# Where y waits for its turn: loading four chunks of y into the halves of four kept tiles, and the first attention gates later

## The chip, the cores and the metric

The kernel runs on one core of one Trainium2 chip. The metric is the device time of one execution in microseconds (us), the median of several runs. Beside it there is one profiled execution, whose trace gives the start and length of every instruction and transfer.

## The reference, cut to what matters

One block of a decoder for 1024 tokens of width 1024, in float32. Only the second branch's projection and what runs beside it matter here:

```python
h = rmsnorm(x, norm_g[l]) * (1.0 + scale[:, None, :]) + shift[:, None, :]
proj = h @ w_in[l]
q, k, v, g_attn, xr, g_rnn, m_attn, m_rnn = jnp.split(proj, SPLIT_POINTS, axis=-1)
...
y_attn = sliding_window_attention_with_sinks(q, k, v, attn_sinks[l]) * jax.nn.silu(g_attn)
y_rnn = rg_lru(xr, ...) * jax.nn.silu(g_rnn)
merged = (jax.nn.sigmoid(m_attn) * (y_attn @ w_attn_proj[l])
          + jax.nn.sigmoid(m_rnn) * (y_rnn @ w_rnn_proj[l]))
x = x + gate[:, None, :] * (merged @ w_out[l])
```

Each float32 operand is written as a high part (rounded to the format that TensorE multiplies) and a low part, the remainder; a product is three: high by high, low by high, high by low.

## The kernel before, in words

The large input projection (`h @ w_in`) is done by pairs of output chunks (`Pair`), each in seven half-size block products (`product`, one per *slot*, 12 matmuls of 128x512), in place of eight. The products' right-hand sides are quarters of h (`hh`, `hl`: high and low parts) and differences of such quarters. The differences' high parts are the eight tiles `nh`, their low parts the four tiles `nl` from the pool `hx` (each 128 partitions x 2 x 1024, 1 MB). A slot uses one half-row of each of the four `nl` tiles: `NT1` (row 0, left half) in slot s+1 of a pair, `T2` (row 1, right) in s+3, `NT3` (row 0, right) in s+6, `NT4` (row 1, left) in s+7 or s+9.

The last slots overlap with the attention. It goes in 32 *units* (u = 0 to 31, one group of four heads by 128 queries each), written by hand in one order for each engine: the unit's scores (`scores`, tiles `s_ps`, from `qs` and `ks`), then one *piece* of other matrix work, then the transposition (`pt`) and the products with v (`pv`) of earlier units. The pieces of units 0 to 5 are the last six slots (s+2 to s+7 of the last pair); from unit 6 on, 32 pieces are the product y @ w_rnn_proj (`rp_steps`, tiles `rp`, matmuls at line 175). Piece i of `rp_steps` runs in unit i+6; pieces 0 and 1 use y's chunks 6 and 7, pieces 2 and 3 chunks 4 and 5, pieces 4 and 5 chunks 0 and 1, pieces 6 and 7 chunks 2 and 3, and from piece 8 on all of them in turn.

What is loaded in that time is asked for on SP's queue, in the order of the code:

- queries and keys: `load_kq(m)` brings `ks` (384 KB) and `qs` (512 KB) for units 2m and 2m+1. There are two places, so the load of m waits for the scores of unit 2m-3; it stands at the end of that unit. kq2 is needed by unit 4, kq3 by unit 6, kq6 by unit 12.
- y: each chunk has a high and a low part (`yh_d`, `yl_d` in HBM, 512 KB each). Chunk 6 and half of 7 stay on the chip, `load_y` brings the rest: 0 and 7 into quarters of h that are used up, 1 to 5 into the pool `ypool`, which is opened in `rp_steps` in the space of h, `nl` and `nh`.
- weights of the projection: `load_r`, two halves `r` of 256 KB. Gates of the attention: `load_gq(m)`, a 256 KB tile `r` of the same ring of six; `a_prep(m)` multiplies it in.

POOL's queue brings the v tiles (`vb`, `vd`) and stores some gates (`smr_d`). SP works in order. Each of its transfers also waits, by a semaphore of eight that go round, for the transfer eight places before it, so at most eight are under way. After the attention, `m_lo`, `mh`, `ml` and later `xo` take `ypool`'s places.

Of the kernel before, what the change touches and what calls it, by code (L numbers as in the profile page):

```python
# [13 lines left out]
F32R = mybir.dt.float32r  # L14
# [4 lines left out]
ALU = mybir.AluOpType  # L19
# [3 lines left out]
P = 128  # L23
S = 1024
D = 1024
KC = 8
HALF = 512
# [18 lines left out]
SL = [slice(0, HALF), slice(HALF, S)]  # L46
# [9 lines left out]
def tile_hybrid_block(ctx, tc, x, pk, rows, posr, posi, c_row, w_ss, w_gate, w_main, w_v,  # L56
                      w_g, w_ap, w_rp, w_out, out):
    nc = tc.nc
    V, A, G, T = nc.vector, nc.scalar, nc.gpsimd, nc.tensor

    def dma(dst, src, eng=nc.sync):
        dst, src = (a.bitcast(F32) if a.dtype == F32R else a for a in (dst, src))
        return eng.dma_start(dst, src)  # L63

    def f32(ap):
        return ap.bitcast(F32)
# [4 lines left out]
    def pool(st, name, bufs=1, **kw):  # L71
        return st.enter_context(tc.tile_pool(name=name, bufs=bufs, reuse_waits="tile", **kw))
# [64 lines left out]
    yh_d = {c: tc.dram_tile([P, S], F32, name=f"yh_d{c}") for c in range(6)}  # L137
# [4 lines left out]


    hba = ctx.enter_context(tc.tile_pool(name="hba", bufs=1))
    h_ctx = ExitStack()
    hb = h_ctx.enter_context(tc.tile_pool(name="hb", bufs=1))
    b12_ctx = ExitStack()
# [10 lines left out]
                lst.append([a[:, SL[0]], a[:, SL[1]]])  # L158
                full.setdefault(kc, []).append(a[:])
    xx = b12_ctx.enter_context(tc.tile_pool(name="xx", bufs=1, side="right"))  # L160
    hx = h_ctx.enter_context(tc.tile_pool(name="hx", bufs=4))
    xall = [hx.tile([P, 2, S], F32, tag="X", name="xT") for i in range(3)]
    xall.append(xx.tile([P, 2, S], F32, name="xT3"))
    xT = [xall[kc % 4][:, kc // 4, :] for kc in range(KC)]
# [390 lines left out]
    B11 = [(hh[i][0], hl[i][0]) for i in range(4)]  # L555
    B21 = [(hh[i + 4][0], hl[i + 4][0]) for i in range(4)]
    B22 = [(hh[i + 4][1], hl[i + 4][1]) for i in range(4)]
    NT1, NT3, NT4, T2 = [], [], [], []

    def differences(i):  # L560
        b11, b12_ = xT[i][:, SL[0]], xT[i][:, SL[1]]
# [5 lines left out]

    def make_operands(i):
        nl = hx.tile([P, 2, S], F32R, tag="X", name="nl")
        for a in range(2):  # L570
            t = i + 4 * a
            A.copy(nh[t][:], xT[t])
            V.tensor_tensor(out=nl[:, a, :], in0=xT[t], in1=f32(nh[t][:]), op=ALU.subtract)
        NT1.append((nh[i][:, SL[0]], nl[:, 0, SL[0]]))
        NT3.append((nh[i][:, SL[1]], nl[:, 0, SL[1]]))
        NT4.append((nh[i + 4][:, SL[0]], nl[:, 1, SL[0]]))
        T2.append((nh[i + 4][:, SL[1]], nl[:, 1, SL[1]]))

    W = {}
# [121 lines left out]
    def at_slot(t, *steps):  # L701

        for i, st_ in enumerate(steps):
            for one in st_ if isinstance(st_, list) else [st_]:
                fixed.setdefault(t + i, []).append(one)
# [744 lines left out]
    def load_r(e):  # L1450
        src = w_rp[e] if e < KC else w_ap[e - KC]
        R[e] = [load_half(src[:, SL[i]]) for i in range(2)]
# [15 lines left out]
                todo.pop(0)()  # L1468

    def load_y(c):  # L1470
        if c == 0:
            yh[c], yl[c] = [[t[i][0] for i in range(2)] for t in (hh, hl)]
            for i in range(2):
                dma(yh[c][i], yh_d[c][:, SL[i]])
                dma(yl[c][i], yl_d[c][:, SL[i]])
            return
        if c >= 6:
            yh[c], yl[c] = [[y_in[c, b][:, t_] for t_ in SL] if (c, b) in y_in else
                            [hh[2 + i][0] for i in range(2)] for b in range(2)]
            if c == 7:  # L1480
                for i in range(2):
                    dma(yl[c][i], yl_d[c][:, SL[i]])
            return
        h_ = W["yp"].tile([P, S], F32R, tag="Y", name="yh")
        l_ = W["yp"].tile([P, S], F32R, tag="Y", name="yl")
        dma(h_[:], yh_d[c])
        dma(l_[:], yl_d[c])
        yh[c] = [h_[:, SL[0]], h_[:, SL[1]]]
        yl[c] = [l_[:, SL[0]], l_[:, SL[1]]]

    def rp_steps():
        h_ctx.close()
        pb_ctx.close()
        psr = pool(ps_ctx, "psr", space=PSUM, side="right")
        rp_acc.extend(psr.tile([P, S], F32, name=f"rp{i}") for i in range(2))
        W["yp"] = pool(ctx, "ypool", bufs=12)
        W["tout"] = pool(ctx, "tout", bufs=1)
        W["hpool"] = pool(ctx, "hpool", bufs=6)

        def part(c, kc2):  # L1500
            for kc in (2 * kc2, 2 * kc2 + 1):
                W["pe"] = mm_k([rp_acc[c % 2][:, t] for t in SL], (O.get((c, 0)), O.get((c, 1))),
                               kc, xh=yh, xl=yl, ends=(6, 3) if c < 2 else (0, KC - 1))

        def finish(c):
            def f():
                flush()
                t = W["tout"].tile([P, S], F32, tag="rp", name="rp32")
                A.copy(t[:], rp_acc[c % 2][:])
                store(tr_d[c], t[:])  # L1510
            later_a.append(f)
            if "att" not in W:
                do_later()

        seq = [(c, k) for k in (3, 2, 0, 1) for c in range(2)]
        seq += [(c, k) for c in range(2, KC) for k in range(4)]
        load_y(4)
        load_y(5)
        for i, (c, k) in enumerate(seq):
            part(c, k)  # L1520
            if i in (1, 2, 3):
                load_y(i)
            if i in (1, 2):
                prep_r(i - 1, 0)
            if i in (6, 10):
                finish(0 if i == 6 else 1)
            if i >= 8 and k == 1 and c > 2:
                finish(c - 1)
            if i % 4 == 2:
                load_r((i + 2) // 4 + 1)  # L1530
            if i >= 4 and i % 4 < 2:
                prep_r((i + 4) // 4, i % 4)
            yield
        finish(7)
# [151 lines left out]
    while W["slot"] < 7 * (len(pairs) - N_ATT) + 1:  # L1686
# [2 lines left out]

    s_last = 7 * len(pairs) - 7  # L1690
    load_y(6)
    at_slot(s_last + 2, ("N", 0, 0, lambda: load_r(0)), ("N", 0, 0, lambda: load_y(7)),
            ("N", 0, 0, lambda: load_r(1)), ("N", 0, 0, lambda: load_y(0)),
            ("N", 0, 0, lambda: prep_r(0, 1)), ("N", 0, 0, lambda: prep_r(1, 1)))

    def fill():
# [23 lines left out]
    for u in range(32 + 3):  # L1720
        todo = (left - KEEP + (35 - u) // 2) // (35 - u)
        if u < 32:
            scores(u)
            maxima_a(u)
            maxima_d(u)
        if 1 <= u < 33:
            weights_a(u - 1)
        low = [steps_[2] for steps_ in high]
        while high:
            high.pop(0)[1]()  # L1730
        for _ in range(todo):
            piece()
        flush()
        if u % 2 and u // 2 + 2 < 16:
            load_kq(u // 2 + 2)
        if 1 <= u < 33:
            weights_d(u - 1)
        if 2 <= u < 34:
            transposed(u - 2)
        if u >= 3:  # L1740
            values(u - 3)
        if 2 <= u < 34:
            split_a(u - 2)
            split_d(u - 2)
        if u >= 3:
            join_a(u - 3)
            join_d(u - 3)
        if u + 1 < 32:
            sink(u + 1)
        while own_stores:  # L1750
            own_stores.pop(0)()
        if 2 <= u < 34:
            masks(u - 2)
        if 3 <= u < 31:
            load_d(u + 1)
            load_v(u + 1)
        if "hpool" in W:
            for f in low:
                f()
            if late and ("gq", late[0]) in U and u >= loaded[late[0]] + 2:  # L1760
                high.append(a_prep(late.pop(0)))
                high[0][0]()
        do_later()
        if u >= 3 and u % 2 == 0:
            late.append((u - 3) // 2)
        if u >= 2 and len(loaded) < 16 and len(loaded) <= (u - 2) // 2 and (
                len(loaded) - (late[0] if late else (u - 2) // 2) < 2):
            m = len(loaded)
            load_gq(m)
            loaded[m] = u  # L1770
# [62 lines left out]
    for c in range(KC):  # L1833
# [24 lines left out]
        if c < 4:  # L1858
            h, l = A11[c]
            A.copy(h, t[:, LEFT])  # L1860
            V.tensor_tensor(out=l, in0=t[:, LEFT], in1=f32(h), op=ALU.subtract)
        else:
            mh, ml = [ypool.tile([P, S], F32R, tag="Y", name=n_) for n_ in ("mh", "ml")]
            for i in SL:
                A.copy(mh[:, i], t[:, i])
            V.tensor_tensor(out=ml[:], in0=t[:], in1=f32(mh[:]), op=ALU.subtract)
            A12.append((mh[:, LEFT], ml[:, LEFT]))
            A22.append((mh[:, RIGHT], ml[:, RIGHT]))
            a11, a21 = [raw[c - 4][:, i] for i in SL]
            a12, a22 = [t[:, i] for i in SL]  # L1870
            V.tensor_tensor(out=a22, in0=a22, in1=a21, op=ALU.add)
            V.tensor_tensor(out=a21, in0=a11, in1=a21, op=ALU.subtract)
            V.tensor_tensor(out=a11, in0=a22, in1=a11, op=ALU.subtract)
            V.tensor_tensor(out=a12, in0=a12, in1=a11, op=ALU.subtract)
# [222 lines left out]
```

## Time and profile before

| what | us |
|---|---|
| runs | 909.71, 909.88, 911.13 (median 909.88) |
| the profiled execution, its time | 909.71 |
| its span, first to last instruction | 908.0 |
| TensorE (PE) busy | 892.6 (98%) |
| VectorE (DVE) busy | 718.5 (79%) |
| ScalarE (ACT) busy | 569.8 (63%) |
| GpSimd (POOL) busy | 186.8 (21%) |
| DMA | 179.79 MB, mean 198 GB/s |
| mean granted TensorE clock | 0.994 |

Times in the trace count from the span's first instruction. Unit 0's scores start at 557.75, unit 6's at 583.56, unit 12's at 618.35. In a timeline row the columns are the start, the length, the engine, the line, the operation with its output and inputs, a count, and in brackets the idle time before it with what ended that. In a window's row stand PE, PEld (weight loads), DVE, ACT and POOL busy in us, the granted clock as a share of full speed, the mean busy share of the 16 DMA engines, and the GB/s that they moved.

### The profile page before, as it was taken

The page shows a single profiled execution, that of the slowest core. Times are in us where ns is not written, and L with a number is a line of the kernel's source. Part 1 is how long each engine was busy: PE and PEld are TensorE (multiplying, and loading weights), DVE is VectorE, ACT ScalarE, POOL GpSimd, SP SyncE. Part 2 cuts the span into 40 slices and gives each one's busy share as a digit, 9 for nine tenths or more (in the row PEclk, how much of TensorE's full clock was granted, in tenths as well). Part 3 has the DMA queues.
Part 4 walks back from the last instruction along what each step waited for, and adds up shares of the span by engine and source line. Part 5 has one row for each costly group of instructions (what it writes and reads, how often), then busy time and mean ns, then how long its engine had stood idle before and what let it go on. Part 6 is the DMA issues. An engine that isn't in the chain of part 4 may idle for free.

```text
span 908.0 us, 12850 instructions
## 1 busy us (share of the span) xinstructions
PE 892.6 (98%) x4314; PEld 747.0 (82%) x4315; DVE 718.5 (79%) x1063; ACT 569.8 (63%) x1099; POOL 186.8 (21%) x330
## 2 busy tenths in 40 slices
PE   9999999999999999999999999997999999999997
PEld 6789888888888888888888888886888888888786
DVE  6998697989679877897897696996999836578855
ACT  7965564655566865777686974885888732115535
POOL 6430241200000000000000002695887720000000
PEclk9999999999999999999999999998999999999999
DMA  9829489863542374265534347997887379416604
GB/s 360 332 94 284 146 258 294 273 212 128 196 163 105 128 251 144 101 229 165 202 112 167 124 137 227 298 344 193 245 237 221 114 263 362 139 47 232 209 1 185
DMA packets 93829, 179.79 MB, mean 198 GB/s; under 512 B 15506, under 2 KB 36002, under 8 KB 93764
## 3 DMA queue, kind: packets, MB, share of 16 engines
q1 hardware_dynamic: 82336, 164.44, 53.0%
q0 software_dynamic: 11280, 14.27, 5.7%
q8 instruction: 34, 0.56, 0.3%
q14 instruction: 31, 0.25, 0.1%
q10 hardware_dynamic: 148, 0.27, 0.1%
HBM read 121.60 MB, written 57.64 MB: 197 GB/s over the span
## 4 chain that ended last, share of the span: by engine, by line
PE 89%; DMA 4%; DVE 3%; ACT 2%; issue 1%; SPq 0%; ACTq 0%
PE bk L714 48%; PE rp L175 13%; PE pgate L1031 5%; PE out L1900 4%; PE pmain L175 4%; PE s_ps L1354 3%; PE pmain L487 2%; PE bk L487 2%; PE pv L1424 2%; DMA yh<-yh_d 2%; DMA qs<-q_d 1%; PE pt L1388 1%; DMA wo<-wo_d 1%; PE pmain L1603 1%; PE pmain L1601 1%; PE pmain L1602 1%
## 5 line engine op out<-in xcount | busy, mean ns | idle before, releaser
L714 PE MATMUL bk<-nh,wh 128*128 128x512 f32 x368 | 143.3, 389 | 0.0
L714 PE MATMUL bk<-nl,wh 128*128 128x512 f32 x368 | 143.2, 389 | 0.0
L714 PE MATMUL bk<-nh,wl 128*128 128x512 f32 x368 | 98.4, 389 | 0.0
L106 ACT CAST wh<-r 128x512 fp32r<-128x512 f32 x107 | 65.5, 618 | 34.1 <-PE pmain L175 10.4
L112 DVE TENSOR_TENSOR wl<-r,wh 128x512 fp32r<-128x512 f32 x91 | 62.1, 691 | 26.2 <-ACT wh L106 26.1
L714 PEld LDWEIGHTS bk<-nh,wl 128*128 128x128 f32 x368 | 69.1, 188 | 14.3
L714 PEld LDWEIGHTS bk<-nl,wh 128*128 128x128 f32 x368 | 69.1, 188 | 14.3
L714 PEld LDWEIGHTS bk<-nh,wh 128*128 128x128 f32 x368 | 69.1, 188 | 14.2
L63 POOL DMA_DIRECT2D yl_d<-it x1 | 0.6, 568 | 349.7 <-DVE it L1114 349.7
L714 PE MATMUL bk<-hl,wh 128*128 128x512 f32 x184 | 71.6, 389 | 0.0
L714 PE MATMUL bk<-hh,wh 128*128 128x512 f32 x184 | 71.6, 389 | 0.0
L112 DVE TENSOR_TENSOR wl<-ws,wh 128x512 fp32r<-128x512 f32 x76 | 51.8, 684 | 6.8 <-ACT wh L106 6.8
L106 ACT CAST wh<-ws 128x512 fp32r<-128x512 f32 x76 | 45.9, 615 | 8.4 <-DVE ws L736 4.1
L1374 ACT ACTIVATE p<-p,small 128x129 f32<-128x129 f32 x128 | 50.0, 396 | 0.0
L714 PE MATMUL bk<-hh,wl 128*128 128x512 f32 x184 | 49.2, 389 | 0.0
L1354 PE MATMUL s_ps<-ks,qs 128*128 128x256 f32 (+1 forms) x256 | 36.5, 286 | 5.2 <-DMA qs<-q_d 5.2
L714 PEld LDWEIGHTS bk<-hl,wh 128*128 128x128 f32 x184 | 34.6, 188 | 7.2
L714 PEld LDWEIGHTS bk<-hh,wl 128*128 128x128 f32 x184 | 34.5, 188 | 7.2
L714 PEld LDWEIGHTS bk<-hh,wh 128*128 128x128 f32 x184 | 34.5, 188 | 7.1
L1354 PEld LDWEIGHTS s_ps<-ks,qs 128*128 128x128 f32 x256 | 33.6, 195 | 6.8 <-issue 5.6
L175 PE MATMUL rp<-yh,wh 128*128 128x512 f32 x112 | 35.8, 402 | 0.0
L714 PE MATMUL bk<-hha,wh 128*128 128x512 f32 x92 | 35.8, 389 | 0.0
(379 smaller groups left out, 2385.3 us busy)
## 6 DMA issues: line engine op xcount, KB each, us to landing
r<-w_main SPq DMA_DIRECT2D x100, 256.0 KB, 4.3
wada<-w_ss SPq DMA_DIRECT2D x16, 512.0 KB, 9.0
qs<-q_d SPq DMA_DIRECT2D x16, 512.0 KB, 8.0
wo_d<-wr SPq DMA_DIRECT2D x28, 256.0 KB, 4.3
wo<-wo_d SPq DMA_DIRECT2D x14, 512.0 KB, 6.6
ks<-k_d SPq DMA_DIRECT2D x12, 384.0 KB, 6.2
xt<-x SPq DMA_DIRECT2D x8, 512.0 KB, 6.9
sma_d<-c SPq DMA_DIRECT2D x16, 256.0 KB, 4.2
```

The costliest lines, as they stand in the source:

```text
L106: A.copy(dst[0][:], src)
L112: eng.tensor_tensor(out=dst[1][:], in0=src, in1=f32(dst[0][:]), op=ALU.subtract)
L175: mm = T.matmul(ps[hf], ww, xx[kc][hf], start=(kc == ends[0] and ww is w_h and xx is xh), stop=(kc == ends[1] and xx is xl))
L487: T.matmul(starts[c][hf], ww[:, c0:c0 + P], xh[kc][hf], start=(kc == 0 and t_ == "h"), stop=(kc == KC - 1 and t_ == "l"))
L714: W["pe"] = T.matmul(ps, ww[:, kc * P:(kc + 1) * P], b[kc][i], start=(first and n == 0), stop=(n == 11), skip_group_check=not first)
L1031: W["pe"] = T.matmul(ps[:, SL[hf]], ww[:, c0:c0 + P], xx_[:, SL[hf]], start=(ic == 0 and i == 0), stop=(ic == 1 and i == 2))
L1354: W["pe"] = T.matmul(o, qs[:, j, qc], ks[:, kb:n % 2 + 2, b, :], start=(b == 0), stop=(b == 1))
L1374: A.activation(px[:, j, :], px[:, j, :], AF.Exp, bias=sm[:, 0, j:j + 1], accum_out=sm[:, 1, j:j + 1])
L1388: W["pe"] = T.transpose(pt[:, :, j, :], px[:, j, 0:P], ident[:])
L1424: W["pe"] = T.matmul(pv[:, cols], w, t_[:, cols], start=(i == 0), stop=(i == len(m) - 1))
L1601: T.matmul(o, hh[kc][th][:, ts_], wh[:, cols], start=(kc == 0), stop=False)
L1900: T.matmul(o, a[k][x_][:, p * P:(p + 1) * P], b[k][y_][:, cols], start=(first and k == 0 and i == 0), stop=(k == 3 and i == 2), skip_group ...
```

## The change: what it does

The pool `hx` is no longer closed at the start of `rp_steps`, so the four `nl` tiles (now also listed as `NL`) stay allocated to the end, and `ypool` has 4 places instead of 12. y's chunk 4 goes into the `NT1` halves, chunk 5 into the `T2` halves, each in four transfers of 256 KB, as soon as the last slot that reads them has run: in units 1 and 2 instead of 6. Chunks 2 and 3 go into the contiguous `NT3` and `NT4` halves, chunk 1 alone into `ypool`. Chunk 7's half is asked for a unit earlier. The attention's gates are asked for two units later up to unit 13, after which two are asked for in units 14 and 15 each. After the attention `mh` and `ml` are in `NL`.

```diff
     hba = ctx.enter_context(tc.tile_pool(name="hba", bufs=1))
+    hx = ctx.enter_context(tc.tile_pool(name="hx", bufs=4))
     h_ctx = ExitStack()
...
-    hx = h_ctx.enter_context(tc.tile_pool(name="hx", bufs=4))
...
         nl = hx.tile([P, 2, S], F32R, tag="X", name="nl")
+        NL.append(nl)
...
     def load_y(c):
-        if c == 0:
-            yh[c], yl[c] = [[t[i][0] for i in range(2)] for t in (hh, hl)]
...
+        if c == 1:
+            both = [W["yp"].tile([P, S], F32R, tag="Y", name="y") for _ in range(2)]
...
+        if c in (2, 3):
+            both = [NL[2 * c - 4 + b][:].rearrange("p a s -> p (a s)")[:, HALF:HALF + S]
+                    for b in range(2)]
...
+        elif c >= 4:
+            yh[c], yl[c] = [[NL[2 * b + i][:, c - 4, SL[c - 4]] for i in range(2)]
+                            for b in range(2)]
+        else:
+            yh[c], yl[c] = [[t[i][0] for i in range(2)] for t in (hh, hl)]
+        for b, (t, d) in enumerate(((yh[c], yh_d), (yl[c], yl_d))):
+            if (c, b) not in y_in:
                 for i in range(2):
...
+                    dma(t[i], d[c][:, SL[i]])
...
-        W["yp"] = pool(ctx, "ypool", bufs=12)
+        W["yp"] = pool(ctx, "ypool", bufs=4)
...
-        load_y(4)
-        load_y(5)
+        load_y(1)
         for i, (c, k) in enumerate(seq):
             part(c, k)
-            if i in (1, 2, 3):
+            if i in (2, 3):
                 load_y(i)
...
-    at_slot(s_last + 2, ("N", 0, 0, lambda: load_r(0)), ("N", 0, 0, lambda: load_y(7)),
-            ("N", 0, 0, lambda: load_r(1)), ("N", 0, 0, lambda: load_y(0)),
+    at_slot(s_last + 2, [ask_y(7), ask_r(0)], ask_y(4), [ask_r(1), ask_y(5)], ask_y(0),
...
-        if u >= 2 and len(loaded) < 16 and len(loaded) <= (u - 2) // 2 and (
+        if u >= 2 and len(loaded) < 16 and len(loaded) <= (u - (4 if u < 14 else 2)) // 2 and (
...
-            mh, ml = [ypool.tile([P, S], F32R, tag="Y", name=n_) for n_ in ("mh", "ml")]
+            mh, ml = [NL[c - 4][:, a, :] for a in range(2)]
```

How SP's queue moves, first in units 1 to 4 (`ga_d3`: a gate's store; `ks`, `qs`: kq2, then kq3; `hha`, `hla`: places in h). Before:

```order
L63 DMA ga_d3_100<-c_5362 128x2x256
L63 DMA hha2_170<-yl_d7_129 128x512
...
L63 DMA ks_5449<-k_d_83 128x768
L63 DMA qs_5451<-q_d0_93 128x1024
L63 DMA r_5493<-w_rp 128x512
...
L63 DMA ga_d3_100<-c_5442 128x2x256
L63 DMA r_5511<-ga_d0_97 128x512
L63 DMA hha0_162<-yh_d0_117 128x512
...
L63 DMA ks_5552<-k_d_83 128x768
L63 DMA qs_5554<-q_d0_93 128x1024
```

The same place now:

```order
L63 DMA ga_d3_100<-c_5362 128x2x256
L63 DMA nl_779<-yh_d4_121 128x512
...
L63 DMA ks_5453<-k_d_83 128x768
L63 DMA qs_5455<-q_d0_93 128x1024
L63 DMA r_5497<-w_rp 128x512
...
L63 DMA nl_779<-yh_d5_122 128x512
...
L63 DMA ga_d3_100<-c_5444 128x2x256
L63 DMA hha0_165<-yh_d0_117 128x512
...
L63 DMA ks_5558<-k_d_83 128x768
L63 DMA qs_5560<-q_d0_93 128x1024
L63 DMA r_5664<-ga_d0_97 128x512
```

Chunk 4 (four transfers, the first is shown) now stands ahead of kq2 where chunk 7's two stood, chunk 5 ahead of kq3, and the first gate (`r<-ga_d0`) behind kq3 instead of ahead of it.

Then the queue from kq4 to kq6, units 5 to 9. Before (of a pair of transfers the first is shown):

```order
L63 DMA ks_5695<-k_d_83 128x512
...
L63 DMA yh_5780<-yh_d4_121 128x1024
...
L63 DMA yh_5784<-yh_d5_122 128x1024
...
L63 DMA r_5837<-ga_d0_97 128x512
L63 DMA yh_5880<-yh_d1_118 128x1024
...
L63 DMA ks_5884<-k_d_83 128x768
...
L63 DMA yh_5957<-yh_d2_119 128x1024
...
L63 DMA r_5961<-w_rp 128x512
...
L63 DMA r_6004<-ga_d0_97 128x512
L63 DMA yh_6035<-yh_d3_120 128x1024
...
L63 DMA ks_6039<-k_d_83 128x768
```

The same place now:

```order
L63 DMA ks_5701<-k_d_83 128x512
...
L63 DMA y_5785<-yh_d1_118 128x1024
...
L63 DMA r_5838<-ga_d0_97 128x512
L63 DMA ks_5881<-k_d_83 128x768
...
L63 DMA nl_779<-yh_d2_119 128x1024
...
L63 DMA r_5954<-w_rp 128x512
...
L63 DMA r_5997<-ga_d0_97 128x512
L63 DMA nl_1144<-yh_d3_120 128x1024
...
L63 DMA ks_6031<-k_d_83 128x768
...
L63 DMA r_6134<-ga_d0_97 128x512
```

Chunks 4 and 5 (2 MB) are gone from between kq4 and kq5, and one gate of 256 KB from ahead of kq6. TensorE's own order of matmuls stays as it is.

More of the change, by code (lines that the diff above doesn't have):

```diff
@@ L557, in tile_hybrid_block @@
     B22 = [(hh[i + 4][1], hl[i + 4][1]) for i in range(4)]
-    NT1, NT3, NT4, T2 = [], [], [], []
+    NT1, NT3, NT4, T2, NL = [], [], [], [], []
     def differences(i):
@@ L1470, in load_y @@
     def load_y(c):
-        if c == 0:
-            yh[c], yl[c] = [[t[i][0] for i in range(2)] for t in (hh, hl)]
-            for i in range(2):
-                dma(yh[c][i], yh_d[c][:, SL[i]])
-                dma(yl[c][i], yl_d[c][:, SL[i]])
+        if c == 1:
+            both = [W["yp"].tile([P, S], F32R, tag="Y", name="y") for _ in range(2)]
+            yh[c], yl[c] = [[t[:, t_] for t_ in SL] for t in both]
+            for t, d in zip(both, (yh_d, yl_d)):
+                dma(t[:], d[c])
+            return
+        if c in (2, 3):
+            both = [NL[2 * c - 4 + b][:].rearrange("p a s -> p (a s)")[:, HALF:HALF + S]
+                    for b in range(2)]
+            yh[c], yl[c] = [[t[:, t_] for t_ in SL] for t in both]
+            for t, d in zip(both, (yh_d, yl_d)):
+                dma(t, d[c])
             return
@@ L1479, in load_y @@
                             [hh[2 + i][0] for i in range(2)] for b in range(2)]
-            if c == 7:
-                for i in range(2):
[L1482 to L1489, printed above, removed]
+        elif c >= 4:
[5 more added lines that the diff above has]
+            if (c, b) not in y_in:
+                for i in range(2):
+                    dma(t[i], d[c][:, SL[i]])
     def rp_steps():
@@ L1691, in tile_hybrid_block, with ask_y, ask_r @@
     load_y(6)
-    at_slot(s_last + 2, ("N", 0, 0, lambda: load_r(0)), ("N", 0, 0, lambda: load_y(7)),
-            ("N", 0, 0, lambda: load_r(1)), ("N", 0, 0, lambda: load_y(0)),
+    def ask_y(c):
+        return "N", 0, 0, lambda: load_y(c)
+    def ask_r(c):
+        return "N", 0, 0, lambda: load_r(c)
+    at_slot(s_last + 2, [ask_y(7), ask_r(0)], ask_y(4), [ask_r(1), ask_y(5)], ask_y(0),
             ("N", 0, 0, lambda: prep_r(0, 1)), ("N", 0, 0, lambda: prep_r(1, 1)))
@@ L1862, in tile_hybrid_block @@
         else:
-            mh, ml = [ypool.tile([P, S], F32R, tag="Y", name=n_) for n_ in ("mh", "ml")]
+            mh, ml = [NL[c - 4][:, a, :] for a in range(2)]
             for i in SL:
                 A.copy(mh[:, i], t[:, i])
-            V.tensor_tensor(out=ml[:], in0=t[:], in1=f32(mh[:]), op=ALU.subtract)
+            V.tensor_tensor(out=ml, in0=t[:], in1=f32(mh), op=ALU.subtract)
             A12.append((mh[:, LEFT], ml[:, LEFT]))
```

## The prediction

> **What bounds the kernel now.** I read the page first. TensorE (PE) is busy for nearly the whole span, so a change that moves no matmul can only win back idle or slowed time of PE:
>
> ```profile
> PE 892.6 (98%) x4314; PEld 747.0 (82%) x4315; DVE 718.5 (79%) x1063; ACT 569.8 (63%) x1099; POOL 186.8 (21%) x330
> ```
>
> So I read PE's waits next. One is worth naming, and it has a transfer behind it; the next in size is at the start of the kernel:
>
> ```profile
> PE s_ps L1354 <- DMA qs<-q_d: 5.2, 1, 5.2
> PE bk L258 <- DVE warm L260: 1.4, 1, 1.4
> ```
>
> The chain of work that ended last (start, length) passes there from PE to the transfers and back. What it names is y's chunk 2, then the queries of kq6:
>
> ```profile
> 588.57 0.97 PE s_ps L1354 x8
> 590.42 14.90 DMA yh<-yh_d
> 605.34 12.88 DMA qs<-q_d
> 618.35 2.05 PE s_ps L1354 x8
> ```
>
> PE's timeline gives the price. These are the scores of units 4, 6, 10, 11, the matmul before the wait, and the scores of units 12, 13 and 14:
>
> ```profile
> 573.85 1.12 PE L1354 MATMUL s_ps<-ks,qs 128*128 128x256 f32 x8
> 583.56 1.12 PE L1354 MATMUL s_ps<-ks,qs 128*128 128x256 f32 x8
> 603.54 1.12 PE L1354 MATMUL s_ps<-ks,qs 128*128 128x256 f32 x8
> 608.40 1.12 PE L1354 MATMUL s_ps<-ks,qs 128*128 128x256 f32 x8
> 612.77 0.40 PE L1424 MATMUL pv<-plc,vb 128*128 128x512 f32 x1
> 618.35 2.05 PE L1354 MATMUL s_ps<-ks,qs 128*128 128x256 f32 x8 [5.18 <-DMA qs<-q_d]
> 625.76 1.12 PE L1354 MATMUL s_ps<-ks,qs 128*128 128x256 f32 x8
> 630.62 1.12 PE L1354 MATMUL s_ps<-ks,qs 128*128 128x256 f32 x8
> ```
>
> A unit takes 4.86 us (603.54 to 608.40, and 625.76 to 630.62). Unit 12 stands idle for 5.18 us (613.17 to 618.35) and then takes 625.76 - 618.35 = 7.41 us, 2.55 more than its neighbours. The granted clock says why (columns: PE, PEld, DVE, ACT, POOL busy, clock, DMA share, GB/s):
>
> ```profile
> 560.00:565.00 5.00, 5.00 (x27) 4.25 (x26) 4.42 (x8) 2.81 (x11) 0.00 (x0) 1.00 0.28 92
> 565.00:570.00 5.00, 5.00 (x33) 4.42 (x32) 4.08 (x9) 4.37 (x14) 0.19 (x1) 1.00 0.98 353
> 570.00:575.00 5.00, 5.00 (x31) 4.38 (x30) 4.40 (x8) 4.33 (x15) 1.17 (x3) 1.00 0.77 241
> 575.00:580.00 5.00, 5.00 (x32) 4.41 (x31) 4.74 (x10) 3.57 (x13) 3.55 (x9) 1.00 0.98 313
> 580.00:585.00 5.00, 5.00 (x33) 4.41 (x32) 4.63 (x9) 4.81 (x16) 4.80 (x8) 1.00 0.79 264
> 605.00:610.00 5.00, 5.00 (x32) 4.46 (x31) 4.79 (x10) 4.20 (x14) 4.76 (x10) 1.00 1.07 328
> 615.00:620.00 5.00, 1.65 (x8) 1.68 (x9) 1.81 (x4) 0.00 (x0) 3.45 (x6) 0.70 1.06 271
> 620.00:625.00 5.00, 5.00 (x19) 4.01 (x18) 2.30 (x4) 2.65 (x10) 0.00 (x0) 0.62 0.68 172
> 625.00:630.00 5.00, 5.00 (x33) 4.46 (x32) 3.32 (x6) 4.14 (x12) 3.18 (x7) 1.00 0.19 78
> ```
>
> The clock is 0.70 and 0.62 of full speed after the wait and 1.00 around it. So the place costs 5.18 + 2.55 = 7.73 us. The same rows show the cause: the DMA engines are full to the end of the wait and nearly empty from 625 on, while at 560 they stood idle (0.28), and they had room at 570 (0.77) and 580 (0.79). SP's queue:
>
> ```profile
> 562.25 0.38 SPq L63 DMA_DIRECT2D ga_d<-c  x1
> 562.73 0.91 SPq L63 DMA_DIRECT2D hha<-yl_d  x2
> 564.16 0.42 SPq L63 DMA_DIRECT2D qs<-q_d  x1
> 564.63 0.90 SPq L63 DMA_DIRECT2D r<-w_rp  x2
> 569.65 0.38 SPq L63 DMA_DIRECT2D ga_d<-c  x1
> 573.66 0.43 SPq L63 DMA_DIRECT2D qs<-q_d  x1
> 580.70 0.42 SPq L63 DMA_DIRECT2D yh<-yh_d  x1
> 599.90 0.33 SPq L63 DMA_DIRECT2D yh<-yh_d  x1
> 605.34 0.32 SPq L63 DMA_DIRECT2D qs<-q_d  x1
> ```
>
> y's chunks 4 and 5 start at 580.70; kq6's queries are asked for only at 605.34, because chunk 3 ahead of them (599.90) had to wait for a place, and they land 12.88 us later, at 618.22.
>
> **The change part by part.** The matmuls are the same ones in the same order, so the span can only fall by the 7.73 us, less what is newly late. Sizes are those of the tiles: a half of y 0.524 MB (a chunk 1.049), kq 0.918, a gate or half weight 0.262.
>
> *Chunks 4 and 5 earlier.* 2.1 MB leave the stretch before kq5 and kq6. Ahead of kq6 the gain is the idle DMA time that is now filled: 0.02 + 0.23 + 0.02 + 0.21 of the four windows from 565 to 585, 5 us each, is 2.4 us, and chunk 7's half, which now goes a unit earlier into the idle 560 to 565, 0.524 MB at 333 GB/s (mean of the two full windows, 353 and 313), 1.6 us. One gate fewer ahead of kq6 is 0.8 us. Sum 4.8 us: kq6 lands at 618.22 - 4.8 = 613.4, needed at 613.17 plus any new lateness before. Counted the other way, from kq3 on, 7.1 MB on SP's queue and some 2 MB on POOL's at about 335 GB/s end near 612. So unit 12's wait goes, but with little in hand; I cost its rest at nothing. What covers it is the next item, since a lateness in unit 6 moves unit 12's need too. Without that cover it is 0.2 us, at worst 2.2 us if half of the idle time isn't filled.
>
> *The price: kq2 and kq3 stand behind more.* Landings before, for kq2's and kq3's queries (issues above; size, us to landing) and for the halves of chunk 7:
>
> ```profile
> qs<-q_d SPq DMA_DIRECT2D x1, 512.0 KB, 5.5
> qs<-q_d SPq DMA_DIRECT2D x1, 512.0 KB, 8.0
> hha<-yl_d SPq DMA_DIRECT2D x2, 256.0 KB, 3.4
> ```
>
> kq2 landed at 564.16 + 5.5 = 569.7. Chunk 4 in place of chunk 7's half adds 0.524 MB, 1.6 us: 571.3, needed at 573.85; hidden by 2.6 us. kq3 landed at 573.66 + 8.0 = 581.7, needed at 583.56. Ahead of it now: chunks 4 and 5 more (2.097), chunk 7's half and one gate fewer (0.786), so 1.31 MB, 3.94 us; filled idle time gives back (0.02 + 0.23 + 0.02) x 5 = 1.35. It lands at 581.7 + 3.94 - 1.35 = 584.3, 0.7 us late. I take 0.7 us. Lower end: 0, at the 353 GB/s of the best window, if the stretch at 570 holds no pause. Upper end: from 569.65 to 581.7, 12 us, six transfers of 256 KB and kq3 (2.75 us) passed with 1.15 us idle, so a quarter cost 1.35 us at most; five net quarters more are 6.75 us, less 1.35 and the 1.9 in hand: 3.5 us late.
>
> *More, smaller transfers.* Chunks 4 and 5 go in eight issues instead of four; SP spends 0.91 us on two, so 1.8 us more of its time in units 1 and 2, where it issued nothing from 565.5 (after `r`) to 569.65. Hidden. Its new waits (PE's slots of units 0 and 1) are over when it gets there. [...]
>
> *Chunks 0 to 3* keep their places in the queue. Chunk 0 stands just ahead of kq3, so by the sum above it lands some 3 us before 584.3, and is needed after 603.54, in unit 10; the others come earlier, as kq6 does: nothing. *Gates later:* `a_prep` of the first moves by up to two units; its product isn't used until after the attention, and nothing of PE waits for it: nothing. It adds one unit with two gates twice, at 14 and 15, 0.26 MB where DMA has 0.19 share. *`mh`, `ml` in `NL`, `ypool` of 4:* the last readers of y end before; the same DVE and ACT work: nothing.
>
> **Sum.** 908.0 - 5.18 - 2.55 + 0.7 = 901.0 of span. The profiled execution took 909.71, 1.7 beside its span: 902.7. The median of the runs is 0.17 above it: **902.9 us**.
>
> The clock's part of that: a wait of 0.7 us is taken at its bare length, while 5.18 us of idleness drew 2.55 more. Were the loss in proportion, 0.34 would be added, 903.2. [...]
>
> **Rivals.**
> 1. *The wait moves to kq3 in unit 6*, or kq6 keeps a part. For it: 0.7 us and 0.2 us are smaller than the errors of such sums. Against: the 5 us before unit 12 are well covered. Waits of 1 to 3.5 us without the slow clock: 904 to 906; with 2.55 us of slow clock, up to 902.0 + 3.5 + 2.55 = 908.0.
> 2. *Nothing changes.* kq6 would still be limited by the eight transfers under way, not by bytes. For it: SP asks for kq6 only 5 us after chunk 3. Against: the DMA share is 1.07 there, so bytes are what the eight wait for. 909.9.
> 3. *Slower: each quarter of y is served nearly by itself.* Place: kq3, unit 6. If a quarter costs q, kq3 is 5q - 1.35 - 1.9 us late, and the kernel is slower when this passes 5.18 (the slow clock being paid again): q above 1.69 us, against 0.79 by bandwidth. At 2.3 us: 8.25 late, 902.0 + 8.25 + 2.55 = 912.8. For it: each landed after 3.4 us; against: at most 1.35 us by the bound.
> 4. *DVE or POOL become the bound* once PE isn't held up: 4.79 and 4.76 of 5 us at 605. Against: units 10 and 11 kept 4.86 us with that, and after 625 both have 3.3 and less. 0.2 us a unit over six units would be 904.
>
> **How the numbers follow.** Forecast (wait gone, new lateness up to 1 us, 902.1 to 903.4): 0.52. Rival 1: 0.26 (a fifth of it with the slow clock). Rival 4: 0.06. Rival 2: 0.10. Rival 3: 0.06. A change of 0.2% (1.8 us, so below 908.1 or above 911.7) is about what a measurement of this kernel can tell. Faster: 0.52 + 0.06 + 0.26 = 0.84. Same: 0.10 of rival 2 and 0.01 of rival 3 (q just above 1.69), 0.11. Slower: 0.05, the rest of rival 3. The range leaves out rivals 2 and 3 and the worst of rival 1: 901.7 to 906.5.
>
> **What would show it.** Right: PE's waits no longer name `qs` with 5.2 us, units 11 to 14 keep 4.86 us, the clock is 1.00 at 615 to 625, the DMA share is near 1 from 565 to 585 and falls before 620, SP asks for kq6 near 600; a first wait for `qs` or `ks` of under a microsecond in unit 6. Wrong: a wait of several us at unit 6 (my queue sum), or at unit 12 still (the eight transfers), or units longer than 4.86 us without a wait for a transfer (DVE or POOL).

## The result, and the profile after

The changed kernel takes 902.87 us, median of 4 runs (901.81 to 903.23), against 910.1 for the kernel before in the same comparison (909.71 to 911.13): a ratio of 0.9922, with an interval of 0.9909 to 0.9934. The forecast was 902.9. The profiled execution took 901.81 us, with a span of 900.1, so 7.9 us less than the span of before.

The engines' busy time, on the page of the changed kernel, and PE's two largest waits:

```profile
PE 889.8 (99%) x4314; PEld 745.0 (83%) x4315; DVE 719.2 (80%) x1063; ACT 569.6 (63%) x1099; POOL 188.0 (21%) x330
...
PE bk L258 <- DVE warm L260: 1.4, 1, 1.4
PE bk L487 <- ACT hha L413: 0.9, 2, 0.7
```

The same 4314 matmuls keep PE busy 2.8 us less (892.6 before). That is matmul time no longer run at the slow clock (before, it read 0.50 of full speed in each us from 617 to 623). The other 5.1 of the 7.9 us is idle time of PE: the wait for `qs` of 5.2 us stood at the top of this list and is now not in it at all. What leads the list was there before and is far from the change.

PE's timeline of the changed kernel, scores of units 4, 6, 11, 12, 13 and 14 (the scores now stand in line 1355):

```profile
573.75 1.12 PE L1355 MATMUL s_ps<-ks,qs 128*128 128x256 f32 x8
583.46 1.12 PE L1355 MATMUL s_ps<-ks,qs 128*128 128x256 f32 x8
608.34 1.12 PE L1355 MATMUL s_ps<-ks,qs 128*128 128x256 f32 x8
613.11 1.22 PE L1355 MATMUL s_ps<-ks,qs 128*128 128x256 f32 x8
618.07 1.12 PE L1355 MATMUL s_ps<-ks,qs 128*128 128x256 f32 x8
622.92 1.12 PE L1355 MATMUL s_ps<-ks,qs 128*128 128x256 f32 x8
```

No start carries a bracket with a wait, and the units from 11 on follow each other at 4.77 to 4.96 us. Unit 14, which began at 630.62, begins at 622.92, 7.7 us earlier, where unit 4 gains only 0.1: nearly all of the gain is made at unit 12. The stretches that the prediction spoke of:

```profile
560.00:565.00 5.00, 5.00 (x27) 4.28 (x26) 4.42 (x8) 2.81 (x12) 0.00 (x0) 1.00 0.38 113
565.00:570.00 5.00, 5.00 (x33) 4.43 (x32) 4.08 (x9) 4.32 (x14) 0.19 (x1) 1.00 0.94 319
570.00:575.00 5.00, 5.00 (x31) 4.34 (x30) 4.41 (x8) 4.38 (x14) 1.28 (x3) 1.00 1.04 391
575.00:580.00 5.00, 5.00 (x32) 4.44 (x31) 4.74 (x10) 3.55 (x14) 3.56 (x9) 1.00 1.05 404
580.00:585.00 5.00, 5.00 (x32) 4.43 (x31) 4.63 (x9) 4.83 (x15) 4.80 (x8) 1.00 1.04 306
...
615.00:620.00 5.00, 5.00 (x33) 4.42 (x32) 4.79 (x10) 3.83 (x13) 4.47 (x8) 1.00 0.71 251
620.00:625.00 5.00, 5.00 (x32) 4.46 (x31) 4.77 (x11) 4.94 (x16) 4.49 (x9) 1.00 0.76 266
```

The clock (third column from the right) stays at 1.00. The DMA share next to it is 1.04 and 1.05 where it had been 0.77 and 0.98, and has room at 615 (0.71), where it had been full (1.06). SP's queue in the changed kernel (chunks 4 and 5, kq3, chunk 3, kq6), and then what kq3 and kq6 took from issue to landing:

```profile
562.62 0.90 SPq L63 DMA_DIRECT2D nl<-yh_d  x2
566.75 1.78 SPq L63 DMA_DIRECT2D nl<-yh_d  x2
575.39 0.32 SPq L63 DMA_DIRECT2D qs<-q_d  x1
594.77 0.45 SPq L63 DMA_DIRECT2D nl<-yh_d  x1
600.15 0.43 SPq L63 DMA_DIRECT2D qs<-q_d  x1
...
qs<-q_d SPq DMA_DIRECT2D x1, 512.0 KB, 7.2
qs<-q_d SPq DMA_DIRECT2D x1, 512.0 KB, 11.8
```

kq3 lands at 575.39 + 7.2 = 582.6 and is needed at 583.46; kq6 is asked for 5.2 us earlier than before, lands at 600.15 + 11.8 = 611.95, and is needed at 613.11. Both come about a microsecond before they are needed, so the new order works with little in hand at two places.

### The profile page after: what moved, and what is told of

Read it like the earlier page. It is cut to its first block, busy times and chain, and to the rows that moved or that the text cites. A ratio compares the mean times of both kernels' runs of the same rounds, so it can differ in the third digit from the quotient of the medians.

```text
span 900.1 us, 12860 instructions
## 1 busy us (share of the span) xinstructions
PE 889.8 (99%) x4314; PEld 745.0 (83%) x4315; DVE 719.2 (80%) x1063; ACT 569.6 (63%) x1099; POOL 188.0 (21%) x330
## 4 chain that ended last, share of the span: by engine, by line
PE 91%; DVE 3%; ACT 2%; DMA 1%; POOL 1%; issue 1%; POOLq 0%; ACTq 0%
PE bk L715 49%; PE rp L175 14%; PE pgate L1032 5%; PE out L1912 4%; PE pmain L175 4%; PE s_ps L1355 3%; PE pv L1425 2%; PE pmain L487 2%; PE bk L487 2%; PE pt L1389 1%; DMA wo<-wo_d 1%; PE pmain L1607 1%; PE pmain L1609 1%; PE pmain L1608 1%; ACT jk L1930 1%
## 5 line engine op out<-in xcount | busy, mean ns | idle before, releaser
L175 PE MATMUL rp<-nl,wh 128*128 128x512 f32 x128 | 37.3, 393 | 0.0
L715 PE MATMUL bk<-hla,wh 128*128 128x512 f32 x92 | 35.8, 389 | 0.0
```

The source lines that it names most:

```text
L175: mm = T.matmul(ps[hf], ww, xx[kc][hf], start=(kc == ends[0] and ww is w_h and xx is xh), stop=(kc == ends[1] and xx is xl))
L715: W["pe"] = T.matmul(ps, ww[:, kc * P:(kc + 1) * P], b[kc][i], start=(first and n == 0), stop=(n == 11), skip_group_check=not first)
```

## The experiments

The theory: the gain is transfer time moved out of the stretch ahead of kq6, and its price falls on kq3 in unit 6. The rivals: it comes from the later gates, from the new places of the chunks, or from a lower number of transfers under way.

**The gates alone**, in the kernel before:

```diff
-        if u >= 2 and len(loaded) < 16 and len(loaded) <= (u - 2) // 2 and (
+        if u >= 2 and len(loaded) < 16 and len(loaded) <= (u - (4 if u < 14 else 2)) // 2 and (
```

> The kernel before, with only the later gates of the change. Theory (bytes ahead of kq6): one gate of 256 KB fewer ahead of kq6, 0.8 us earlier, so unit 12 still waits about 4.4 us and the clock still drops: 908.9 to 909.4. Rival (the gates' delay is what frees the queue): the wait is gone, about 903.

908.61 us (10 runs) against 909.68, ratio 0.9992 (0.9979 to 1.0006), a little below the 908.9 to 909.4 that were expected. The timeline of this kernel at unit 12, and the stretch after it:

```profile
616.49 2.04 PE L1354 MATMUL s_ps<-ks,qs 128*128 128x256 f32 x8 [3.55 <-DMA qs<-q_d]
...
615.00:620.00 5.00, 3.51 (x13) 3.24 (x14) 2.26 (x5) 1.43 (x6) 3.44 (x5) 0.66 1.05 311
```

In this profile the wait is 1.6 us shorter, and the slow clock stays; over the runs nothing is left that can be measured. The gates alone don't carry the gain.

**The early chunks alone**: the changed kernel with the gates' old condition.

```diff
-        if u >= 2 and len(loaded) < 16 and len(loaded) <= (u - (4 if u < 14 else 2)) // 2 and (
+        if u >= 2 and len(loaded) < 16 and len(loaded) <= (u - 2) // 2 and (
```

> The changed kernel with the gates asked for as early as before. Theory: one gate more ahead of kq3 and of kq6, 0.8 us each; in the changed kernel's trace kq3 lands 0.9 us and kq6 1.2 us before they are needed, so both are now just in time: waits of 0 to 0.3 us, 902.9 to 903.5. Rival (the gates matter): a wait of several us in unit 6 or 12, 904 to 909.

903.67 us (901.81 to 906.34, 8 runs), ratio 0.9943 (0.9927 to 0.9958). So the early chunks, with chunk 7's half, bring about three quarters of the gain: 0.57% of 0.78%. What the gates add to them, about 0.2%, is no more than these runs can tell, since the two intervals overlap; where it comes from shows in unit 6 of this kernel:

```profile
585.65 1.18 PE L1355 MATMUL s_ps<-ks,qs 128*128 128x256 f32 x8 [1.13 <-DMA qs<-q_d]
```

kq3 comes 1.13 us too late; with the gates later, unit 6 has no wait. The expectation had put this wait at 0.3 us at most.

**The places alone**: the chunks lie where the changed kernel has them, and all loads are asked for when the kernel before asked.

```diff
-        load_y(1)
+        load_y(4)
+        load_y(5)
...
-            if i in (2, 3):
+            if i in (1, 2, 3):
...
-    at_slot(s_last + 2, [ask_y(7), ask_r(0)], ask_y(4), [ask_r(1), ask_y(5)], ask_y(0),
+    at_slot(s_last + 2, ask_r(0), ask_y(7), ask_r(1), ask_y(0),
...
-        if u >= 2 and len(loaded) < 16 and len(loaded) <= (u - (4 if u < 14 else 2)) // 2 and (
+        if u >= 2 and len(loaded) < 16 and len(loaded) <= (u - 2) // 2 and (
```

> The changed kernel's places (the nl tiles kept, chunks 2 to 5 in their halves, ypool of 4, mh and ml in NL) with every load asked for when it was before. Theory: places cost and bring nothing; the wait of 5.2 us in unit 12 and the slow clock are back, 909.7 to 910.5. Rival (the places themselves free something): about 903.

910.21 us (10 runs), ratio 1.0012 (1.0 to 1.0023). Two waits on the timeline of this kernel:

```profile
604.52 1.19 PE L1355 MATMUL s_ps<-ks,qs 128*128 128x256 f32 x8 [1.21 <-DMA qs<-q_d]
...
618.90 1.80 PE L1355 MATMUL s_ps<-ks,qs 128*128 128x256 f32 x8 [4.67 <-DMA qs<-q_d]
```

The old wait is back, in two pieces. The freed halves are worth nothing by themselves; they only allow the earlier asking.

**One chunk early instead of two**: chunk 5 goes back to the start of `rp_steps`.

```diff
-    at_slot(s_last + 2, [ask_y(7), ask_r(0)], ask_y(4), [ask_r(1), ask_y(5)], ask_y(0),
+    at_slot(s_last + 2, [ask_y(7), ask_r(0)], ask_y(4), ask_r(1), ask_y(0),
...
+        load_y(5)
         load_y(1)
```

> The changed kernel with chunk 5 asked for only at the start of rp_steps, behind kq4, as before; chunk 4 stays early. Theory: 1.05 MB, 3.1 us, come back ahead of kq6, which then lands about 1.9 us late; a wait of 1.9 us without slow clock, 904.8. If the slow clock is in proportion to the wait (2.55 for 5.18), 905.7. Rival (it takes one chunk only to free the queue): 902.9.

904.22 us (903.35 to 905.4, 6 runs), ratio 0.9947 (0.9928 to 0.9966). Unit 12 of this kernel and the stretch after it:

```profile
614.26 1.19 PE L1355 MATMUL s_ps<-ks,qs 128*128 128x256 f32 x8 [1.28 <-DMA qs<-q_d]
...
615.00:620.00 5.00, 5.00 (x33) 4.46 (x33) 4.22 (x9) 2.92 (x11) 4.18 (x7) 1.00 0.97 309
```

With one chunk a wait of 1.28 us remains (1.9 was expected), and the clock stays at 1.00 behind it. The first chunk, with chunk 7's half and the gates, brings most of the gain, since it also ends the slow clock.

**Bytes or places among the transfers under way?** The kernel before, in which chunks 4 and 5 load only their left half: as many transfers, half their bytes.

```diff
+        if c >= 4:
+            dma(h_[:, SL[0]], yh_d[c][:, SL[0]])
+            dma(l_[:, SL[0]], yl_d[c][:, SL[0]])
+            yh[c], yl[c] = [[t[:, SL[0]]] * 2 for t in (h_, l_)]
+            return
```

> The kernel before, in which the transfers of chunks 4 and 5 bring only the left half of each (the right half's products use the left half again; so part of the input is left out). As many transfers at the same places, 1.05 MB fewer. Theory (bytes): kq6 lands 3.1 us earlier, unit 12 waits 2.0 us, the clock stays full: 904.2. Rival (the eight transfers under way are what limits, whatever their size): 909 to 910.

904.03 us (903.55 to 905.82, 5 runs), ratio 0.9949 (0.9931 to 0.9966). Unit 12 of this kernel, and its clock in stretches of 1 us:

```profile
614.51 1.57 PE L1354 MATMUL s_ps<-ks,qs 128*128 128x256 f32 x8 [1.98 <-DMA qs<-q_d]
...
614.00:615.00 1.00, 0.49 (x4) 0.52 (x5) 1.00 (x3) 0.33 (x1) 0.60 (x2) 1.00 1.02 253
615.00:616.00 1.00, 1.00 (x7) 1.00 (x7) 0.95 (x3) 0.00 (x0) 0.94 (x3) 0.55 1.09 311
616.00:617.00 1.00, 1.00 (x4) 0.81 (x3) 0.51 (x2) 0.88 (x4) 1.00 (x2) 0.50 1.05 294
617.00:618.00 1.00, 1.00 (x3) 0.72 (x3) 0.90 (x2) 1.00 (x7) 0.94 (x2) 0.50 1.05 326
618.00:619.00 1.00, 1.00 (x5) 0.79 (x4) 0.95 (x3) 0.77 (x3) 0.38 (x1) 0.74 1.06 276
619.00:620.00 1.00, 1.00 (x7) 0.80 (x6) 0.19 (x1) 0.00 (x0) 0.00 (x0) 1.00 0.68 169
```

The wait falls from 5.18 to 1.98 us, so 3.2 us for 1.05 MB, which is 328 GB/s. The number of transfers was kept, so bytes set the wait. One thing was not expected: after a wait of only 1.98 us the clock was halved for some 3.4 us (0.45 + 0.50 + 0.50 + 0.26 us of full speed lost, 1.71).

**How near is unit 6 to the edge?** The changed kernel with one, two or four more transfers of 512 KB each (from HBM to HBM) on SP's queue ahead of kq3:

```diff
+    more_d = [tc.dram_tile([P, S], F32, name=f"more_d{i}") for i in range(1)]
+
+    def ask_more():
+        return "N", 0, 0, lambda: [dma(d, w_rp[7]) for d in more_d] and None
...
-    at_slot(s_last + 2, [ask_y(7), ask_r(0)], ask_y(4), [ask_r(1), ask_y(5)], ask_y(0),
+    at_slot(s_last + 2, [ask_y(7), ask_r(0)], ask_y(4), [ask_r(1), ask_y(5), ask_more()], ask_y(0),
```

> The changed kernel with one more transfer of 512 KB (from HBM to HBM, unused) on SP's queue between chunk 5 and chunk 0, so ahead of kq3. Theory: 0.524 MB at 333 GB/s are 1.6 us; kq3 had 0.9 us in hand, so unit 6 waits 0.7 us, the clock stays full: 903.6. Rival (kq3 is not near its limit): no wait, 902.9.

> The same with two such transfers, 1.05 MB. Theory: kq3 3.15 us later, a wait of 2.3 us in unit 6 (or less in unit 12 with it), clock full: 905.2. If the slow clock is in proportion to a wait: 906.3.

> The same with four such transfers, 2.1 MB. Theory: kq3 6.3 us later, a wait of 5.4 us in unit 6 and, as it is as long as the one of the kernel before, some 2.5 us of slow clock: 910.8. Rival (each transfer also holds one of the eight places, so the queue stalls further): above 912.

With one: 904.44 us, ratio 0.9956 (0.9935 to 0.9977). With two: 909.39, 0.9999 (0.9988 to 1.0011). With four: 911.58, 1.0029 (1.0015 to 1.0043). The timeline of the kernel with one (units 6 and 12):

```profile
585.11 1.19 PE L1355 MATMUL s_ps<-ks,qs 128*128 128x256 f32 x8 [0.80 <-DMA qs<-q_d]
...
614.58 1.19 PE L1355 MATMUL s_ps<-ks,qs 128*128 128x256 f32 x8 [0.42 <-DMA qs<-q_d]
```

Unit 6 of the kernel with two, and the stretches after it:

```profile
588.95 2.05 PE L1355 MATMUL s_ps<-ks,qs 128*128 128x256 f32 x8 [4.47 <-DMA qs<-q_d]
...
585.00:590.00 5.00, 1.05 (x5) 1.08 (x6) 1.86 (x4) 1.59 (x4) 4.72 (x9) 0.70 1.06 311
590.00:595.00 5.00, 5.00 (x18) 4.06 (x18) 2.80 (x5) 3.29 (x11) 0.45 (x1) 0.62 0.94 309
```

And unit 6 of the kernel with four:

```profile
594.36 2.05 PE L1355 MATMUL s_ps<-ks,qs 128*128 128x256 f32 x8 [10.18 <-DMA qs<-q_d]
```

One transfer cost about what was expected in unit 6 (a wait of 0.8 us, against 0.7); unit 12 waits another 0.42 us, and the median is 0.8 us above the expected 903.6. Two and four cost twice what was expected: 4.47 us against 2.3, and 10.18 against 5.4. So the price in unit 6 is real, and two more transfers give back the whole gain. These copies go from HBM to HBM, which the loads of the change don't, so the next run asks the same of plain loads.

**The same with loads of y**: chunk 4's four transfers are issued a second time ahead of kq3, 1.05 MB.

```diff
-    at_slot(s_last + 2, [ask_y(7), ask_r(0)], ask_y(4), [ask_r(1), ask_y(5)], ask_y(0),
+    at_slot(s_last + 2, [ask_y(7), ask_r(0)], ask_y(4), [ask_r(1), ask_y(5), ask_y(4)], ask_y(0),
```

> The changed kernel with chunk 4's four transfers issued a second time behind chunk 5 (the same data into the same places): 1.05 MB of plain loads ahead of kq3, in place of the transfers from HBM to HBM of the earlier test, which delayed kq3 more than their bytes. Theory (333 GB/s): kq3 3.15 us later, 0.9 in hand, a wait of 2.3 us in unit 6; with no slow clock 905.2, with one stretch of 3.4 us at half clock, as a wait of 2.0 us drew in the half-bytes kernel, 906.9. Rival (extra transfers cost more than their bytes, 2.9 us per 512 KB): a wait of 5 us and 909.5 or more.

909.9 us (10 runs), ratio 1.0013 (1.0003 to 1.0024). Unit 6 of this kernel, kq3 on SP's queue and its time to landing, and the stretches around it:

```profile
590.92 2.05 PE L1355 MATMUL s_ps<-ks,qs 128*128 128x256 f32 x8 [5.48 <-DMA qs<-q_d]
...
580.42 0.32 SPq L63 DMA_DIRECT2D qs<-q_d  x1
...
qs<-q_d SPq DMA_DIRECT2D x1, 512.0 KB, 10.4
...
585.00:590.00 5.00, 0.45 (x4) 0.24 (x3) 2.79 (x6) 2.42 (x5) 4.79 (x9) 1.00 1.05 316
590.00:595.00 5.00, 4.08 (x15) 3.67 (x16) 1.27 (x2) 1.99 (x9) 1.36 (x2) 0.66 1.04 335
```

Plain loads cost as much as the copies did, as the rival had it: kq3 goes from 0.9 us early to 5.48 late, 6.4 us for 1.05 MB, where the rate of 333 GB/s gives 3.1. The two halves of it can be read: SP issues kq3 5.0 us later (580.42 for 575.39), and it then takes 3.2 us longer (10.4 for 7.2), while its own need moved by 2.0 us (590.92 - 5.48 = 585.44 for 583.46). The later need is not the second loading's doing: unit 3 already starts 1.8 us later (570.90 for 569.08), before chunk 4 is asked for again at 572.83; what made it later the runs don't show. Taken off the 5.0 us, it leaves 3.0 for the later asking, which is what the rate gives for 1.05 MB. What the rate doesn't give is the other half, the 3.2 us. The DMA engines are full throughout (shares of 1.09 and 1.05 in the two windows from 580 to 590). Between kq3's issue and its landing SP's queue moved 3.01 MB and POOL's 0.31 (13.7% of the engines' time), against 2.26 and 0.38 (17.7%) in the changed kernel, so it was not POOL's queue that held kq3 up. SP's own next transfers came nearer: kq4 was asked for 2.0 us after kq3 (582.43) in place of 4.4 (579.75), y's chunk 1 3.2 us after it in place of 5.2. That these share the engines with kq3 while it is under way would fit; no run holds them back, so it isn't shown.

**Chunk 5 asked for only after kq3**, in the changed kernel, to give unit 6 more in hand:

```diff
-    at_slot(s_last + 2, [ask_y(7), ask_r(0)], ask_y(4), [ask_r(1), ask_y(5)], ask_y(0),
-            ("N", 0, 0, lambda: prep_r(0, 1)), ("N", 0, 0, lambda: prep_r(1, 1)))
+    at_slot(s_last + 2, [ask_y(7), ask_r(0)], ask_y(4), ask_r(1), ask_y(0),
+            [ask_y(5), ("N", 0, 0, lambda: prep_r(0, 1))], ("N", 0, 0, lambda: prep_r(1, 1)))
```

> The changed kernel with chunk 5 asked for two units later, behind kq3 instead of ahead of it (still ahead of kq4). Theory: kq3 gets 3.1 us more in hand; kq6 keeps its place in the sum, since the DMA engines stay busy; as PE no longer waits for kq3 or kq6 in the changed kernel's trace there is nothing more to win but the odd late run: 902.0 to 902.9, within 0.1% of the changed kernel. Rival (the 3.1 us are idle again before kq6): a wait of up to 2 us in unit 12, 903 to 905.

902.46 us (901.89 to 902.81, 4 runs), ratio 0.9922 (0.9907 to 0.9937), with the changed kernel at 902.58 on the same chip: no difference. kq3 lands at 579.4 here, 3.7 us before its need in place of 0.9, and nothing is won by that. Its one wait for `qs` is in unit 12, as PE's waits show:

```profile
PE s_ps L1355 <- DMA qs<-q_d: 0.4, 1, 0.4
```

**The changed kernel once more**, unchanged, beside that.

> The changed kernel once more, beside the one with chunk 5 behind kq3 on the same chip. Theory: 902.9 as before, with no wait for queries or keys above 0.5 us.

902.58 us (902.18 to 902.95, 4 runs), ratio 0.9924 (0.9909 to 0.9939). Unit 12 of this second profile of it, kq6 on the queue, and its time to landing:

```profile
613.97 1.20 PE L1355 MATMUL s_ps<-ks,qs 128*128 128x256 f32 x8 [1.23 <-DMA qs<-q_d]
...
599.77 0.43 SPq L63 DMA_DIRECT2D qs<-q_d  x1
...
qs<-q_d SPq DMA_DIRECT2D x1, 512.0 KB, 14.1
```

kq6 lands at 613.9 here, 1.2 us late, where the first profile had it 1.2 us early. The expectation of no wait above 0.5 us missed: unit 12 is just in time in one execution and just late in another. That is worth about a microsecond, and the runs of this kernel lie that far apart.

## Why the prediction was right

**What goes.** Right: the wait and the slow clock at unit 12, 5.18 + 2.55 = 7.73 us, are gone; unit 14 starts 7.7 us earlier. With the early asking and the gates given back the kernel takes 910.21 again, with the gates alone given back 903.67, so it is the early asking that carries most of the gain.

**kq6 4.8 us earlier.** Right: 6.3 us in one profile (618.2 to 611.95), 4.3 in the other (613.9). "With little in hand" was right too; its rest, costed at nothing, was 0 and 1.23 us. The cover that the prediction named, a lateness in unit 6, wasn't there. Chunk 7's half went elsewhere than it said: it was asked for at 555.39, so the DMA share from 555 to 560 rose from 0.61 to 0.88, while 560 to 565 stayed low (0.28 before, 0.38 now). No run moves this half alone, so its 1.6 of the 4.8 us is not shown by itself.

**kq3 0.7 us late.** This term, the only price in the sum, was mis-sized: kq3 came 0.9 us early, beyond even the lower end of 0, with no wait in unit 6 in either profile. The step that failed is the rate. By 333 GB/s kq3 should have landed 2.6 us later than before; it landed 0.9 us later (581.7 to 582.6). From 570 to 580 the engines moved 391 and 404 GB/s, 3.98 MB, where 333 would be 3.33; the 0.65 MB between them are 1.9 us. The mean of two full windows of the kernel before was no ceiling. What made the rate higher there the runs don't tell. The 0.7 us and the rest at kq6 are nearly of one size, so the sum hardly felt it.

**The number.** That 902.9 met the median of 902.87 so closely is luck. The sum's span was 901.0, the two profiles have 900.1 and 901.2; and the sum put the median 0.17 us above the profiled execution, where it came out 1.06 above it (902.87 - 901.81). A price that was too high and a difference that was too small nearly cancel. What the working does bear out is the size of what goes, 7.73 us.

**Eight smaller transfers.** Right. By the prediction's own formula a quarter cost (0.9 + 1.35) / 5 = 0.45 us, far from the 1.69 at which the kernel would have been slower. With quarters queued back to back the highest rates of these stretches were reached, 391 and 404 GB/s from 570 to 580.

**Gates and places at nothing.** The places: right (1.0012). The gates: half right. Alone they show no gain (0.9992), but without them kq3 is 1.13 us late. The prediction had them in kq3's bytes and not as a term of their own.

**The clock.** Taking a short wait at its bare length was the author's estimate, and it was right: behind waits of 0.80, 1.13, 1.23 and 1.28 us no first matmul group took longer than 1.20 us, and the clock read 1.00 in the stretches behind each of them. The other reading in the prediction, loss in proportion to the wait, fell. But it doesn't take a wait as long as the 5.18 us of before: with half the bytes 1.98 us of waiting drew the slow clock (0.50 of full speed from 616 to 618).

**The rivals.** Rival 1, a wait that moves to kq3 or stays at kq6, came about as far as 1.23 us in one profile. Rival 2, the eight transfers, fell: half the bytes in the same number of transfers shortened the wait by 3.2 us. Rival 3, quarters served nearly one by one, fell at 0.45 us a quarter; a loss by way of kq3 there can be, but it takes another megabyte ahead of kq3 to lose everything (909.39 and 909.9). Rival 4 fell: units keep 4.8 to 5.0 us with DVE at 4.79 of 5.

## What to carry to other kernels

Where a transfer lands late although its queue runs full, look further back for stretches in which the DMA engines stood idle, and ask which later load could go there and what buffer it would need: here free halves of dead tiles were enough to take out 7.7 us. Price such a move at the first transfer that now stands behind it, and leave that one a microsecond or two: one more megabyte there would have cost all of the gain. Count a short wait of TensorE bare (here up to 1.28 us), but a longer one with the slow clock that can come with it (here it came with each of the seven waits from 1.98 to 10.18 us).

## What the runs showed of the hardware

The slow clock was not in proportion to the wait. The seven profiles with longer waits read as follows (waits in us from the span's start; the granted clock in the 5 us windows from the times named, with 1.00 in the windows next to them); the last column is how many us of full speed these windows lost:

| kernel | wait | granted clock | lost |
|---|---|---|---|
| before | 613.17 to 618.35 | 0.70 from 615, 0.62 from 620 | 3.4 |
| gates alone | 612.94 to 616.49 | 0.66 from 615 | 1.7 |
| places alone | 614.23 to 618.90 | 0.92 from 615, 0.74 from 620 | 1.7 |
| half the bytes | 612.53 to 614.51 | 0.66 from 615 | 1.7 |
| two copies | 584.48 to 588.95 | 0.70 from 585, 0.62 from 590 | 3.4 |
| four copies | 584.18 to 594.36 | 0.83 from 585, 0.50 from 590, 0.65 from 595 | 5.1 |
| chunk 4 twice | 585.44 to 590.92 | 0.66 from 590 | 1.7 |

So 1.7 us were lost with waits of 1.98, 3.55, 4.67 and 5.48 us, 3.4 with 4.47 and 5.18, and 5.1 with 10.18. The length of the wait alone does not set the loss; what else does, the runs don't show.

In the kernel before the part of the slow stretch that lay inside the wait cost nothing more: the clock read 0.50 from 616.95 to 623.78, so for 6.8 us, of which 1.4 lay inside the wait; half of the other 5.4 is 2.7, near the 2.55 of the prediction.

The same bytes did not cost the same ahead of every load. Ahead of kq6 1.05 MB cost 3.2 us, near the 3.1 of the 333 GB/s. Ahead of kq3 1.05 MB less (chunk 5 behind it) brought 2.8 us, but 1.05 MB more cost 6.4 us as loads, and 0.9 + 4.47 = 5.4 as copies. The DMA engines were full up to the end of these three waits (shares in the 5 us windows in which they lie: 1.01 with half the bytes, 1.05 and 1.04 with chunk 4 twice, 1.07 and 1.06 with two copies). Of the 6.4 us, about half is the later asking, and the other half kq3's longer time from issue to landing.
